# A causal convolution over matrices: the MID node's data sums on GpSimd, and x loaded into SBUF throughout

## Chip, cores and metric

The kernel runs on one core of one Trainium2 chip. The metric is the device time of one execution in microseconds, the median of its runs; lower is better. A core has TensorE (PE, matrix products), VectorE (DVE) and ScalarE (ACT) for elementwise work, GpSimd (POOL), SyncE (SP), and 16 DMA engines that all queues share. Each engine works through its own instructions in the order of the program, and waits on semaphores for the others.

## What is computed

```python
B, S, D, K = 8, 4096, 512, 8      # x: B,S,D   kernel: K,D,D   all float32
out = np.zeros_like(x)
for k in range(K):
    shifted = x moved down by k positions in S, zeros in front
    out += np.matmul(shifted, kernel[k])
```

Every output row is the sum of eight products of an input row with a 512x512 matrix.

## The kernel before

**Layout.** The 32768 rows are cut into 128 runs of 256 consecutive rows, one run per partition. A step takes K = 8 positions of every run, so there are 32 steps (i = 0 to 31). Products need the data transposed, with the 512 features on partitions: XT holds one step, positions 0 to 3 in its lower half and 4 to 7 in its upper half.

**Fewer products.** The convolution of eight taps is not done with 64 position-by-tap products per step. It is split three times into halves, and each split replaces four smaller products by three: one for the low part (LO), one for the high part (HI) and one for the sum of both (MID). A step so has three nodes, MID, LO and HI, and each node has nine products of 128x512 by 512x512 (four matmuls each). In return sums of data and of weights are needed. The weight sums are made once. The data sums are made in each step in bf16: D4, D41, D42, D421 for LO and HI, and D1, D2, D21 for the MID node. The last three are eleven blocks of 128x512: D1 two, D2 five, D21 four.

**Who makes the sums.** `tt` (L75) issues an add on VectorE. `prep_m` (L100) makes D1 and D2[1:5] from XT, `prep_d27` (L105) makes D2[0] = XT[5] + XT[7], and `prep_d21` (L108) makes D21 from D2. At the time of `prep_m` the upper half of XT still holds the step before and the lower half already holds the new one.

**How x arrives.** `load_x` (L86) loads one half step from DRAM, float32, cast to bf16, on GpSimd's DMA queue. In steps 0 to 2 it goes into SBUF tiles `xin` of a pool of two buffers. From step 3 on it goes into DRAM tiles `xd`. `transpose_x` (L91) is a DMA transpose on SP's queue from that tile into a half of XT.

**The order.** It is written out by hand (`manual_schedule`): the first six nodes, those of steps 0 and 1, line by line, and the rest (steps 2 to 31, 90 nodes) in the loop at the end. In the loop a node `cur` does its leaf products `node_l`, the earlier stages of the next node `nxt` (`node_a0`, `node_u`, `node_seed`, `node_dts`, `node_v`, `node_d`) are woven in, and `node_a1` of the node after that closes the pass. `node_l` of a MID node reads D21, `node_a1` and `node_a0` read D1, `node_u` reads XT[0] and `node_v` reads D2. `node_e` ends a node: for MID ScalarE copies the result into `ms`, for LO and HI VectorE adds or subtracts it into `y`, and SP stores `y`. The transposes of the next step stand at the start of MID (lower half) and at the end of LO (upper half), and the two loads for the step after that stand right behind the latter:

```python
        if a == LO and more:
            transpose_x(i + 1, 1)
            if i + 2 < NIT:
                load_x(i + 2, 0)
                load_x(i + 2, 1)
```

In XT, transposes wait for the readers of the half that they overwrite; the upper half is read by `prep_m`, `prep_d27` and `prep_d4`.

Of the kernel before, what the change touches and what calls it, by code (L numbers as in the profile page):

```python
# [22 lines left out]
def kernel(  # L23
# [6 lines left out]
    nc = tc.nc  # L30
    B, S, D = x.shape
    K = kernel.shape[0]
    P = 128
# [5 lines left out]
    bf = mybir.dt.bfloat16  # L39
# [12 lines left out]
    xpool = ctx.enter_context(tc.tile_pool(name="x", bufs=2))  # L52
# [22 lines left out]
    def tt(o, a, b, op):  # L75
        nc.vector.tensor_tensor(out=o, in0=a, in1=b, op=op)  # L76


    def load(out, src):
        nc.gpsimd.dma_start(out=out, in_=src)  # L80

    xin = {}

    dpool = ctx.enter_context(tc.tile_pool(name="xd", bufs=6, space=bass.MemoryType.DRAM))

    def load_x(i, h):  # L86
        pool = xpool if i < 3 else dpool
        xin[i, h] = pool.tile([P, 4, D], bf, name="xin" if i < 3 else "xd")
        load(xin[i, h], xr[:, K * i + 4 * h:K * i + 4 * h + 4, :])

    def transpose_x(i, h):  # L91
        nc.sync.dma_start_transpose(  # L92
            out=XT[:, 4 * h:4 * h + 4, :].rearrange("p j (c m) -> p (j c) m", m=P),
            in_=xin[i, h].rearrange("p j d -> p (j d)"))


    def pairs(z):
        return z.rearrange("p (a b) d -> p a (b d)", b=2)

    def prep_m():  # L100

        tt(D1[:, 0:2], XT[:, 7::-7], XT[:, 0:2], ADD)
        tt(pairs(D2[:, 1:5]), pairs(XT)[:, 3::-3], pairs(XT)[:, 0:2], ADD)

    def prep_d27():  # L105
        tt(D2[:, 0], XT[:, 5], XT[:, 7], ADD)

    def prep_d21():  # L108
        tt(D21[:, 0:4], D2[:, 0:4], D2[:, 1:5], ADD)

    def prep_d4(h):
        a, b = (XT[:, 4:8], XT[:, 0:4]) if h == LO else (XT[:, 0:4], XT[:, 4:8])
        tt(D4[:, 4 * h:4 * h + 4], a, b, ADD)

    def prep_d41(h):
        if h == LO:
            tt(D41[:, 0:2], D4[:, 7::-7], D4[:, 0:2], ADD)
        else:
            tt(D41[:, 2:4], D4[:, 3:5], D4[:, 4:6], ADD)

    def prep_d42(h):
        if h == LO:
            tt(pairs(D42)[:, 0:2], pairs(D4)[:, 3::-3], pairs(D4)[:, 0:2], ADD)
        else:
            tt(D42[:, 4:8], D4[:, 2:6], D4[:, 4:8], ADD)

    def prep_d421(h):
        if h == LO:
            tt(D421[:, 0:4:2], D42[:, 7:0:-6], D42[:, 0:4:2], ADD)
            tt(D421[:, 1:4:2], D42[:, 0:4:2], D42[:, 1:4:2], ADD)  # L130
        else:
            tt(D421[:, 4:8], D42[:, 3:7], D42[:, 4:8], ADD)
# [11 lines left out]
    H, HF = XT, D421.bitcast(f32).rearrange("p (t b) d -> p t (b d)", b=2)  # L144
    nc.sync.dma_start(out=HF, in_=xr[:, RUN - 4:RUN, :])
    load_x(0, 0)
    zero = spool.tile([P, D], bf, name="zero")
    nc.vector.memset(zero, 0.0)  # L148
# [90 lines left out]
    def node_a1(k):  # L239
        n = Node()  # L240
        nodes.append(n)
        n.k, (n.i, n.a) = k, order[k]
        a = n.a
        n.s = streams(n.i, a)
        n.q = pair(3)
        product(n.q[:, 1], n.s[1][1], W[a, MID, HI], True)
        nc.scalar.copy(out=n.q[:, 0], in_=n.q[:, 1])  # L247
        n.p = {}

    def node_a0(n):  # L250
        product(n.q[:, 0], n.s[1][0], W[n.a, MID, LO], False)

    def node_u(n):
        product(n.q[:, 1], n.s[0], W[n.a, MID, MID], False)

    def node_seed(n, b_):
        n.p[b_] = pair((2 * n.k + b_) % 3)
        if b_ == LO:
            nc.scalar.copy(out=n.p[b_][:, 1], in_=n.q[:, 1])  # L259
        else:  # L260
            nc.scalar.mul(out=n.p[b_][:, 1], in_=n.q[:, 1], mul=-1.0)  # L261

    def node_dts(n):
        n.dts = cpool.tile([P, D], f32, name="dts")
        nc.scalar.copy(out=n.dts, in_=n.q[:, 0])  # L265

    def node_v(n, b_):
        product(n.p[b_][:, 1], n.s[2][b_], W[n.a, b_, MID], False)

    def node_d(n, b_):  # L270
        p = n.p[b_]
        if b_ == LO:
            tt(p[:, 0], n.dts, p[:, 1], SUB)
        else:
            nc.vector.scalar_tensor_tensor(out=p[:, 0], in0=p[:, 1], scalar=-1.0,  # L275
                                           in1=n.dts, op0=MUL, op1=SUB)
# [3 lines left out]
    def node_l(n, b_, j):  # L280
        product(n.p[b_][:, j], n.s[3][2 * b_ + j], W[n.a, b_, j], False)
# [11 lines left out]
    def node_e(n, b_):  # L293
        p = n.p[b_]
        if n.k < 4:
            pool, name = ((mpool, "ms"), (ypool, "y"), (fpool, "f"), (ypool, "y"))[n.k]
            y = pool.tile([P, 2, D], f32, name=name)
            nc.scalar.copy(out=y, in_=p)
            first[n.i, n.a, b_] = y
        elif n.a == MID:  # L300
            ms[b_] = mpool.tile([P, 2, D], f32, name="ms")
            nc.scalar.copy(out=ms[b_], in_=p)  # L302
        else:
            y = ypool.tile([P, 2, D], f32, name="y")
            if b_ == HI and n.k == len(order) - 1:

                for j, eng in enumerate((nc.scalar, nc.sync)):
                    tt(y[:, j], p[:, j], ms[b_][:, j], ADD if n.a == LO else SUB)
                    eng.dma_start(out=orr[:, K * n.i + 4 * n.a + 2 * b_ + j, :], in_=y[:, j])
            else:  # L310
                tt(y, p, ms[b_], ADD if n.a == LO else SUB)
                store(n.i, n.a, b_, y)
# [54 lines left out]
    transpose_pe("he", 1, H, 1, 4)  # L367
    load_w(7)
    load_x(0, 1)
    nc.vector.tensor_copy(out=XF[:, 6:8], in_=bank["xb"])  # L370
    tt(D2, XF[:, 1:6], XF[:, 3:8], ADD)
    fill(pair(2))
    tt(D4[:, 2:4], XF[:, 2:4], XF[:, 6:8], ADD)
    load_x(1, 0)
    direct(0, 2)
    tt(to(E4[:, 1:4]), prev(bank["he"]), to(XF[:, 1:4]), ADD)
# [47 lines left out]
    node_u(nodes[1])  # L424
    node_e(nodes[0], 0)
    prep_d27()
    mid_dve(2, HI, LO)
    load_w(1)
# [88 lines left out]
    node_l(nodes[4], 0, LO)  # L517
    node_u(nodes[5])
    prep_m()
    node_d(nodes[4], 1)  # L520
    node_y(nodes[4], 0, LO)
# [8 lines left out]
    node_dts(nodes[5])  # L530
    node_v(nodes[5], 0)
    prep_d27()
    node_seed(nodes[5], 1)
    node_y(nodes[4], 1, LO)
# [42 lines left out]
    for k, (i, a) in enumerate(order):  # L577
        if k < 6:
            continue
        cur = nodes[k]  # L580
        more = i + 1 < NIT
        if a == MID and more:
            transpose_x(i + 1, 0)
        node_l(cur, 0, LO)
        node_l(cur, 0, HI)
        nxt = nodes[k + 1] if k + 1 < len(order) else None
        if nxt:
            node_a0(nxt)
            node_u(nxt)
        node_l(cur, 1, LO)  # L590
        node_e(cur, 0)
        if nxt:
            node_seed(nxt, 0)
            node_seed(nxt, 1)
            node_dts(nxt)
        if a == MID:
            prep_d421(LO)
            prep_d41(HI)
        elif a == LO:
            if more:  # L600
                prep_m()
            prep_d421(HI)
        elif more:
            prep_d41(LO)
            prep_d42(LO)
            prep_d21()
        if nxt:
            for b_ in range(2):
                node_v(nxt, b_)
                node_d(nxt, b_)  # L610
        if a == MID:
            prep_d42(HI)
            prep_d27()
        elif more:
            prep_d4(LO if a == LO else HI)
        node_l(cur, 1, HI)
        if k + 2 < len(order):
            node_a1(k + 2)
        node_e(cur, 1)
# [5 lines that stand above are left out]
# [30 lines left out]
```

## Time and profile before

| | before |
|---|---|
| median of 2 runs | 900.64 us (900.48 and 900.81) |
| the profiled execution | 900.81 us |
| its span | 898.7 us |
| mean granted clock of PE | 0.935 |
| PE busy | 771.2 us (86%) |
| VectorE busy | 658.0 us (73%) |
| ScalarE busy | 285.0 us (32%) |
| GpSimd busy | 41.4 us (5%) |
| DMA issues of xd | 58 of 512 KB |
| DMA transposes of XT | 3 from xin, 58 from xd |

The span runs from the first to the last instruction; the time includes what lies around it. Busy shares are means over the whole span, so they hide that stages differ; the row of 40 slices (each 22.5 us) and tables by stage show that. In a group's row the number behind the bar is the busy time in us and then the mean of one instruction in ns; behind the second bar stands the engine's idle time just before these instructions, with what ended it. A wait is written "who <- for whom: total us, times, longest us". "PEclk" is the clock that TensorE was granted, as a share of the full one.

### The profile page before, as it was taken

Reading aid. Unit: us, or ns where it says so; the run is one execution under the profiler, and the core shown is the slowest. Engines: PE = TensorE matmul, PEld = TensorE weight load, DVE = VectorE, ACT = ScalarE, POOL = GpSimd, SP = SyncE. Lnnn points to the kernel's source line nnn. Section 1 sums busy time; section 2 is a strip of 40 time slices with the busy share of each in tenths; the row PEclk is TensorE's granted clock in tenths of the full one; section 3 lists DMA queues with packets and bytes.
Section 4 is the critical chain, followed back from the end, with each engine's and each line's share of the span. In section 5 each row is a group of like instructions: output and inputs, shape, how many; then the busy total and the mean of one; then the engine's idle time right before and its main releaser. Section 6 shows DMA issues by size and latency. Waiting matters only on the chain.

```text
span 898.7 us, 9321 instructions
## 1 busy us (share of the span) xinstructions
PE 771.2 (86%) x3513; PEld 349.1 (39%) x3584; DVE 658.0 (73%) x766; ACT 285.0 (32%) x462; POOL 41.4 (5%) x80
## 2 busy tenths in 40 slices
PE   7980813106999999999999999999999999999997
PEld 3430301002444444444444444444444444444443
DVE  4970802006888888888888888888888888888886
ACT  3640200001333333333333333333333333333332
POOL 4032121110000000000000000000000000000000
PEclk9995865656999999999999999999999999999999
DMA  9999999999554444444455544454545444445553
GB/s 203 189 186 211 235 210 249 239 211 212 141 140 140 125 128 129 135 132 128 139 141 140 141 141 131 128 140 141 141 129 151 129 137 135 128 131 141 140 132 127
DMA packets 159374, 139.42 MB, mean 155 GB/s; under 512 B 130145, under 2 KB 134241, under 8 KB 159201
## 3 DMA queue, kind: packets, MB, share of 16 engines
q1 hardware_dynamic: 145456, 99.89, 40.1%
q0 software_dynamic: 13728, 38.67, 22.0%
q8 instruction: 28, 0.46, 0.2%
q10 hardware_dynamic: 144, 0.26, 0.1%
q14 instruction: 18, 0.14, 0.1%
HBM read 77.33 MB, written 97.52 MB: 195 GB/s over the span
## 4 chain that ended last, share of the span: by engine, by line
PE 75%; DMA 12%; another core or an unknown queue 5%; DVE 4%; SPq 2%; issue 1%; POOL 0%; ACT 0%; DVEq 0%; ACTq 0%; POOLq 0%
PE pp L200 74%; DMA XT<-xin 5%; DMA out_dram<-y 4%; DMA xin<-in_x_dram 2%; DVE D L76 2%; DMA XT<-xd 2%; DVE y L76 1%; SPq L92 1%; SPq L285 1%; DVE pp L76 0%; DVE pp L275 0%; POOL w L80 0%; ACT pp L259 0%; PE pp L189 0%
## 5 line engine op out<-in xcount | busy, mean ns | idle before, releaser
L200 PE MATMUL pp<-w,D 128*128 128x512 bf16 x3214 | 718.2, 381 | 88.8 <-DVE D L76 80.9
L200 PEld LDWEIGHTS <-D 128*128 128x128 bf16 x3280 | 321.7, 98 | 479.0 <-DVE D L76 84.0
L76 DVE TENSOR_TENSOR D<-XT 128x2048 bf16<-128x2048 bf16 (+2 forms) x153 | 142.4, 947 | 134.6 <-DMA XT<-xd 70.3
L76 DVE TENSOR_TENSOR D<-D 128x1024 bf16<-128x1024 bf16 (+1 forms) x252 | 228.4, 947 | 1.6 <-ACT D L356 1.6
L76 DVE TENSOR_TENSOR y<-pp,ms 128x1024 f32<-128x1024 f32 (+1 forms) x121 | 146.7, 1213 | 51.4 <-PE pp L200 44.0
L247 ACT COPY pp<-pp 128x512 f32<-128x512 f32 x95 | 54.1, 570 | 338.7 <-PE pp L200 335.9
L259 ACT COPY pp<-pp 128x512 f32<-128x512 f32 x95 | 54.1, 570 | 207.7 <-PE pp L200 196.1
L76 DVE TENSOR_TENSOR pp<-dts,pp 128x512 f32<-128x512 f32 x95 | 65.8, 692 | 34.8 <-ACT dts L265 33.1
L302 ACT COPY ms<-pp 128x1024 f32<-128x1024 f32 x60 | 61.0, 1016 | 33.1 <-PE pp L200 32.0
L275 DVE SCALAR_TENSOR_TENSOR pp<-pp,dts 128x512 f32<-128x512 f32 x95 | 66.1, 696 | 3.3
L265 ACT COPY dts<-pp 128x512 f32<-128x512 f32 x95 | 57.5, 605 | 2.0 <-PE pp L200 2.0
L261 ACT ACTIVATE pp<-pp 128x512 f32<-128x512 f32 x95 | 56.1, 590 | 2.7 <-DVE y L76 2.7
L80 POOL DMA_DIRECT2D xd<-in_x_dram x58 | 30.3, 552 | 122.5 <-DMA xd<-in_x_dram 117.5
L200 PE MATMUL pp<-w,F 128*128 128x512 bf16 x34 | 9.8, 413 | 28.5 <-DVE pp L275 28.4
L200 PE MATMUL pp<-w,XT 128*128 128x512 bf16 x118 | 30.6, 380 | 0.3 <-issue 0.2
L76 DVE TENSOR_TENSOR w<-w,w 128x2048 bf16<-128x2048 bf16 x18 | 21.7, 1222 | 0.3 <-DMA w<-in_kernel_dram 0.3
L200 PEld LDWEIGHTS <-XT 128*128 128x128 bf16 x120 | 11.8, 99 | 14.5 <-issue 0.7
L200 PEld LDWEIGHTS <-F 128*128 128x128 bf16 x36 | 3.8, 104 | 33.5 <-issue 30.0
L200 PE MATMUL pp<-w,w 128*128 128x512 bf16 x36 | 9.0, 378 | 1.3 <-ACT pp L247 0.7
L183 PE MATMUL pp<-zero 128*128 128x512 bf16 x23 | 8.0, 479 | 2.4 <-DVE zero L148 1.2
L341 DVE MEMSET D<- 128x64 bf16 x2 | 0.2, 112 | 8.1 <-ACT D L354 7.6
L80 POOL DMA_DIRECT2D w<-in_kernel_dram x8 | 6.1, 770 | 0.6 <-DMA w<-in_kernel_dram 0.6
(56 smaller groups left out, 75.2 us busy)
## 6 DMA issues: line engine op xcount, KB each, us to landing
out_dram<-y SPq DMA_DIRECT2D x123, 512.0 KB, 3.3
xd<-in_x_dram POOLq DMA_DIRECT2D x58, 512.0 KB, 21.2
w<-in_kernel_dram POOLq DMA_DIRECT2D x8, 512.0 KB, 15.9
xin<-in_x_dram POOLq DMA_DIRECT2D x6, 512.0 KB, 13.6
D<-in_x_dram SPq DMA_DIRECT2D x1, 1024.0 KB, 4.8
out_dram<-ms SPq DMA_DIRECT2D x2, 512.0 KB, 18.4
out_dram<-f SPq DMA_DIRECT2D x2, 512.0 KB, 20.7
XT<-xd SPq DMA_TRANSPOSE x58, 5.4
```

Of the source, the lines that this page charges most:

```text
L76: nc.vector.tensor_tensor(out=o, in0=a, in1=b, op=op)
L80: nc.gpsimd.dma_start(out=out, in_=src)
L92: nc.sync.dma_start_transpose(out=XT[:, 4 * h:4 * h + 4, :].rearrange("p j (c m) -> p (j c) m", m=P), in_=xin[i, h].rearrange("p j d -> p ...
L183: nc.tensor.matmul(pw[:, h], lhsT=zero[:, 0:P], rhs=zero, start=True, stop=True)
L200: nc.tensor.matmul(bank, lhsT=comp[:, c * P:(c + 1) * P], rhs=w[:, c, :], start=start and c == 0, stop=c == DC - 1, skip_group_check=True)
L247: nc.scalar.copy(out=n.q[:, 0], in_=n.q[:, 1])
L259: nc.scalar.copy(out=n.p[b_][:, 1], in_=n.q[:, 1])
L261: nc.scalar.mul(out=n.p[b_][:, 1], in_=n.q[:, 1], mul=-1.0)
L265: nc.scalar.copy(out=n.dts, in_=n.q[:, 0])
L275: nc.vector.scalar_tensor_tensor(out=p[:, 0], in0=p[:, 1], scalar=-1.0, in1=n.dts, op0=MUL, op1=SUB)
L285: nc.sync.dma_start(out=orr[:, t0:t0 + 2, :], in_=y)
L302: nc.scalar.copy(out=ms[b_], in_=p)
```

## The change

Two edits. First, the DRAM pool is gone and all loads of x go to the SBUF tiles `xin` (two buffers). Second, in the loop `prep_m`, `prep_d21` and `prep_d27` are called with `tg`, which issues the same add on GpSimd; in the first six nodes they stay on VectorE. The place of each call in the order is kept.

```diff
-    dpool = ctx.enter_context(tc.tile_pool(name="xd", bufs=6, space=bass.MemoryType.DRAM))
-
     def load_x(i, h):
-        pool = xpool if i < 3 else dpool
-        xin[i, h] = pool.tile([P, 4, D], bf, name="xin" if i < 3 else "xd")
+        xin[i, h] = xpool.tile([P, 4, D], bf, name="xin")
         load(xin[i, h], xr[:, K * i + 4 * h:K * i + 4 * h + 4, :])
...
-    def prep_m():
-
+    def tg(o, a, b, op):
+        nc.gpsimd.tensor_tensor(out=o, in0=a, in1=b, op=op)
+
+    def prep_m(tt=tt):
         tt(D1[:, 0:2], XT[:, 7::-7], XT[:, 0:2], ADD)
...
-    def prep_d27():
+    def prep_d27(tt=tt):
...
-    def prep_d21():
+    def prep_d21(tt=tt):
...
             if more:
-                prep_m()
+                prep_m(tg)
             prep_d421(HI)
         elif more:
             prep_d41(LO)
             prep_d42(LO)
-            prep_d21()
+            prep_d21(tg)
...
         if a == MID:
             prep_d42(HI)
-            prep_d27()
+            prep_d27(tg)
```

## Prediction

> **What bounds the kernel now.** I read the page's 40 slices first. One slice is 22.5 us.
>
> ```profile
> PE   7980813106999999999999999999999999999997
> ...
> DVE  4970802006888888888888888888888888888886
> ...
> POOL 4032121110000000000000000000000000000000
> PEclk9995865656999999999999999999999999999999
> DMA  9999999999554444444455544454545444445553
> ```
>
> There are two kernels in this row. From slice 11 (225 us) to the end PE is full at the full clock, VectorE is at 80 to 89%, GpSimd is empty and the DMA engines are half used: that part is bound by PE. Before it, in slices 4 to 10, PE is mostly idle while the DMA engines are saturated. The waits of the first 240 us (who <- whom: total, times, longest) say for whom PE idled:
>
> ```profile
> PE pp L200 <- DVE D L76: 80.9, 2, 46.9
> DVE D L76 <- DMA XT<-xin: 64.2, 2, 34.8
> ...
> DVE D L76 <- DMA XT<-xd: 50.5, 2, 48.7
> ...
> PE pp L200 <- DVE pp L275: 28.4, 1, 28.4
> ```
>
> PE waits for VectorE's sums, and these wait for the DMA transposes that fill XT. Together with two small waits of PE (1.3 us for ACT L261, 1.2 us for DVE L76) that is 111.8 us. Why the transposes are late stands in the timeline of that stretch (start, duration, engine):
>
> ```profile
> 39.37 27.97 SPq L92 DMA_TRANSPOSE XT<-xin  x2
> ...
> 44.09 1.23 DVE L76 TENSOR_TENSOR D<-XT 128x2048 bf16<-128x2048 bf16 x1
> ...
> 45.62 3.47 POOL L80 DMA_DIRECT2D xd<-in_x_dram  x6
> ...
> 197.91 0.52 POOL L80 DMA_DIRECT2D xd<-in_x_dram  x1 [2.15 <-DMA xd<-in_x_dram]
> ```
>
> From 45.62 to 197.91 us GpSimd issues all 58 loads into xd, one each 2.67 us, as fast as they land: nothing makes a load wait for the step that uses it. The transpose issued at 39.37, before this flood, has landed when VectorE reads XT at 44.09: 4.7 us. Those issued in the flood took up to 60 us.
>
> Next, one steady step. Time zero of a step is the copy L247 at 502.20, at which PE turns from HI to MID:
>
> ```profile
> 502.20 0.57 ACT L247 COPY pp<-pp 128x512 f32<-128x512 f32 x1 [2.80 <-PE pp L200]
> ...
> 505.75 2.46 SPq L92 DMA_TRANSPOSE XT<-xd  x1
> ...
> 517.99 1.22 DVE L76 TENSOR_TENSOR y<-pp,ms 128x1024 f32<-128x1024 f32 x1
> ...
> 519.67 3.21 SPq L92 DMA_TRANSPOSE XT<-xd  x1
> ```
>
> The lower half's transpose leaves 3.5 us into the step; the upper half's leaves 17.5 us into it, behind the store of y (517.99) on SP's queue. Where VectorE waited for it, it landed 5.6 us (566.93 to 572.51), 5.7 us and once 7.4 us after its issue. The step lasts 23.37 us (SP's y stores from 512.90 to 863.51: 15 steps), each of its three nodes 7.8 us.
>
> **The change, part by part.**
>
> *No xd buffers.* All loads go back to the two SBUF buffers xin, one for each half. A load must now wait until the transpose of the step before has read its buffer, so the flood can't form, and the first six steps' transposes should land as the one at 39.37 did. That returns the 111.8 us of PE's idling, and the slow clock after each idle stretch: PE restarts at a granted clock of 0.5, for 4.2 us (93.5 to 97.7), 5.9 us (149.4 to 155.3) and some 7 busy us (208.5 to 217), of which half is lost, 8.5 us. 898.7 - 111.8 - 8.5 = 778 us would be the span with a steady loop as now. VectorE stood idle in all of these waits, so I expect little to appear behind them; if the three early transposes showed 5 us each, it would be 793.
>
> *VectorE loses four instructions a step*: D2[0] (0.42 us), D1 (0.68), D2 (1.22) and D21 (1.22), 3.5 us of some 20. In the steady loop PE sets the pace, so this is worth nothing.
>
> *GpSimd gets them, in the order of the program.* Its queue per step becomes D2[0], D1, D2, load of the lower half, load of the upper half, D21. The price is not in the trace. Its nearest rows:
>
> ```profile
> L76 DVE TENSOR_TENSOR D<-D 128x2048 bf16<-128x2048 bf16 x123 | 147.4, 1218 | 0.0
> ...
> masks.py:199 POOL TENSOR_SCALAR_AFFINE_SELECT ident<-ident 128x128 bf16<-128x128 bf16 x1 | 0.3, 287 | 0.1
> ```
>
> Floor: VectorE's 1.22 us for the same shape. From GpSimd's own row: 16 x 287 ns = 4.6 us if all of it scales, 3.1 us if the 98 ns of a one-element memset there are fixed (98 + 16 x 189). That select reads one operand and the sum reads two, so I take the upper end, 4.6 us; D1 then costs 2.3, D2[0] 1.15, in all 12.65 us a step.
>
> The Trainium skill (GPSIMD Engine Reference, Performance versus the Vector engine) gives 4497 ns for a two-input add of 2048 float32 elements per partition, about twice VectorE; with that in place of 4.6 us, the sum below would be 3 us lower. No run here has shown it yet.
>
> *D2[0], D1 and D2 are covered.* With the lower half's transpose as now (landed 9 us into the step) D1 ends at 11.3 and D2 at 15.9. D1 is first used by PE at 14.7, D2 in the HI node (20), and the upper half's transpose, which may not overwrite XT[7] before D2 has read it, leaves at 17.5. If that cover of 1.6 us is gone, each us more is a us per step.
>
> *D21 is not covered: this is the new wait.* The load of the upper half, for two steps ahead, waits on GpSimd for the upper half's transpose to land. Behind it in the queue stands D21, and PE's first product of the next MID node reads D21. Before, VectorE made D21 early in the HI node, waiting for nothing of this. The new chain from one MID start to the next: 17.5 (transpose issued) + 5.6 (landed) + 0.55 (load issued; xin row 0.57, median 0.54) + 4.6 (D21) = 28.25 us against 23.37. PE idles 4.9 us in each step, and as the chain starts at PE's MID node again, it repeats; nothing catches up. The last loads are issued in step 29, so MID nodes 3 to 30 wait: 28 times.
>
> *The clock.* What an idle PE costs after the wait, the trace shows in rows of 1 us (length, PE, PEld, DVE, ACT, POOL, granted clock):
>
> ```profile
> 65.00:66.00 1.00, 0.17 (x1) 0.00 (x0) 0.00 (x0) 0.00 (x0) 0.52 (x1) 1.00 1.07 211
> ...
> 69.00:70.00 1.00, 0.00 (x0) 0.00 (x0) 0.00 (x0) 0.00 (x0) 0.00 (x0) 0.98 1.06 209
> 70.00:71.00 1.00, 0.00 (x0) 0.00 (x0) 0.00 (x0) 0.00 (x0) 0.16 (x1) 0.50 1.08 214
> ```
>
> PE stops at 65.2 and the clock halves at 70.0: 4.8 us. At the two other stalls it took 2.5 us (115.4 to 117.9) and 3.8 us (161.7 to 165.5). A gap of 4.9 us is just over all three. A halved clock costs 2.1 us (4.2 at half) to 2.9 us (5.9 at half); I take 2.5 us in three gaps of four, 1.9 us a step; bounds 0 and 2.9.
>
> *Sum.* 28 x (4.9 + 1.9) = 190 us; 778 + 190 = 968 us of span. The profiled execution took 900.81 us for a span of 898.7, so 2 us lie around it, and it is 0.2 us over the median of the runs: 970 us.
>
> A rule that speaks against the change beyond this: the Trainium skill (SBUF — State Buffer, Who interferes with whom) says that a VectorE instruction with two SBUF inputs and a GpSimd instruction that reads SBUF exclude each other, the later one waiting for the whole of the earlier. VectorE's D4 sum of the upper half is released by the same transpose as GpSimd's load, so D21 would start after its 1.22 us instead of 0.55 us; by that rule the time would be 28 x 0.67 = 19 us more, 989. No row of before has both engines reading, so the trace can't say.
>
> **The rivals.**
>
> *GpSimd's sum is cheap (faster).* All hangs on D21's price. At VectorE's 1.22 us the chain is 24.9 us, 1.5 us over the step, too short to halve the clock: 778 + 28 x 1.5 + 2 = 822 us. At 3.1 us PE idles 3.4 us, which one of the three stalls would have punished: 28 x (3.4 + 0.8) gives 898. Break-even is (900.6 - 780) / 28 = 4.3 us per step, clock included. For it: 287 ns is one short instruction with its start in it. Against it: two operands. Faster by over 2% needs a price below about 2.6 us, or a transpose from SBUF that lands at 4.6 us together with a price below 3.6.
>
> *GpSimd and VectorE hold each other up (slower still).* VectorE reads two SBUF operands for over 8 us of each step and GpSimd would for 12.65. If they don't overlap, D21 starts at least 0.7 us later, every gap halves the clock, and D2's cover is eaten: 28 x (4.9 + 0.7 + 2.5) gives 1007 us. Against: the sum of some 21 us still fits into a step of 30.
>
> *PE keeps its clock (about the same to slower).* If 4.9 us are not enough, as the 4.8 us at 65 us nearly were, 28 x 4.9 gives 917 us.
>
> *The loop stays bound by PE (faster).* If the load didn't hold GpSimd's queue, D21 would be early and the time 780 us. In the program built from the changed kernel the load stands ahead of D21 with a wait for that transpose, so I give this little.
>
> **How the numbers follow.** My forecast (930 to 990) 0.46; both engines hold each other up 0.23; clock kept 0.13; GpSimd cheap 0.14; loop bound by PE 0.04. A change of 2% is about what a measurement of this kernel can tell from none; it is 883 to 919 us here. Faster by over 2%: 0.15 (most of the cheap case, and the last). Within 2%: 0.11 (half of the clock's case, the rest of the cheap one). Slower by over 2%: 0.74. The range for eight in ten, 890 to 1020, reaches from a price near 3 us to both engines in each other's way.
>
> **What would show it.** Right: GpSimd busy near half of the loop; the xin loads spread over the whole span; slices 4 to 10 full for PE; then one gap of some 5 us per step, "PE waits for POOL D21", in front of each MID node; a period near 30 us; PEclk below 9 all along. D21's row near 4600 ns decides the price. Wrong: PE at 99% in the loop with no wait for GpSimd, or a time below 883 us; also a loop that waits for D1 or for the transpose of the lower half, or PE idle before 225 us as now.

## The result

The changed kernel takes 989.46 us (median of 2 runs, 988.8 and 990.13) against 900.64 us before: a ratio of 1.0986, 95% interval 1.0939 to 1.1033, so 10% slower. Its span is 987.0 us. The start and the loop changed in opposite directions, as the prediction said. The slices of the changed kernel, now 24.7 us each:

```profile
PE   7999688988879888899788898888888889888898
...
DVE  5999679667676766866677766776777776677766
...
POOL 3103534345433454234542345523455233552450
PEclk9999789988899888998888988889888898888989
DMA  9966676456565565645657446574565655557533
```

PE and its clock are full in slices 2 to 4 (to 99 us); the old kernel began to idle at 65 us. From slice 5 on PE is below 90% in 29 of 36 slices, its granted clock falls with it, and GpSimd works throughout. The waits from 90 us to the end say what PE waits for:

```profile
PE pp L199 <- POOL D L98: 129.3, 28, 8.8
PEld L199 <- issue: 99.8, 365, 0.3
```

PE waited 28 times for a GpSimd sum, 4.6 us each on average. The second row is the slow clock: weight loads that follow each other too late, at the half clock's pace, 13 in each step. One step in the timeline of the changed kernel (selected rows):

```profile
498.01 3.20 SPq L89 DMA_TRANSPOSE XT<-xin  x1
...
503.06 1.23 DVE L76 TENSOR_TENSOR D<-XT 128x2048 bf16<-128x2048 bf16 x1
503.50 0.53 POOL L80 DMA_DIRECT2D xin<-in_x_dram  x1 [14.73 <-PE pp L199]
504.05 4.15 POOL L98 TENSOR_TENSOR D<-D 128x2048 bf16<-128x2048 bf16 x1
...
504.20 1.22 DVE L76 TENSOR_TENSOR y<-pp,ms 128x1024 f32<-128x1024 f32 x1
505.33 5.57 DVE L76 TENSOR_TENSOR D<-D 128x1024 bf16<-128x1024 bf16 x3
...
508.25 21.05 PE L199 MATMUL pp<-w,D 128*128 128x512 bf16 x82 [4.26 <-POOL D L98]
...
528.50 3.24 SPq L89 DMA_TRANSPOSE XT<-xin  x1
...
534.01 0.53 POOL L80 DMA_DIRECT2D xin<-in_x_dram  x1 [15.01 <-PE pp L199]
```

This is the chain of the prediction, row by row: the upper half's transpose (498.01), the load that had to wait for it (503.50), D21 behind the load (504.05 to 508.20), PE's first MID product (508.25), and 20.25 us later the next transpose. The profile names PE as the load's releaser here, but the transpose is the better reading: the load starts 0.44 us after VectorE's D4 sum, which reads what the transpose wrote, and in the first gap, where the profile names the transpose for both, the distance is the same (D4 at 105.73, the load at 106.18). From the transpose at 130.17 to the one at 958.40, 27 steps, a step lasts 30.68 us.

The granted clock of the same gap, in rows of 1 us (the clock is the third number from the end):

```profile
506.00:507.00 1.00, 0.00 (x0) 0.00 (x0) 1.00 (x1) 0.00 (x0) 1.00 (x1) 0.99 1.11 205
507.00:508.00 1.00, 0.00 (x0) 0.00 (x0) 1.00 (x1) 0.00 (x0) 1.00 (x1) 0.50 0.99 193
...
513.00:514.00 1.00, 1.00 (x4) 0.35 (x3) 0.00 (x0) 0.00 (x0) 1.00 (x1) 0.59 0.00 0
```

PE stopped at 503.99. The clock fell 3.0 us later and came back at 513.8, so PE worked 5.6 us at half speed.

VectorE's three sums at 505.33 take 5.57 us here and 1.89 us in the old kernel. The groups say the same in the mean (ns of one behind the busy time); first the old kernel's row, then the changed kernel's:

```profile
L76 DVE TENSOR_TENSOR D<-D 128x1024 bf16<-128x1024 bf16 x127 | 81.8, 684 | 1.6 <-ACT D L356 1.6
```

```profile
L76 DVE TENSOR_TENSOR D<-D 128x1024 bf16<-128x1024 bf16 x127 | 184.9, 1493 | 1.6 <-ACT D L355 1.6
...
L98 POOL TENSOR_TENSOR D<-D 128x2048 bf16<-128x2048 bf16 x29 | 121.0, 4174 | 0.5
L98 POOL TENSOR_TENSOR D<-XT 128x2048 bf16<-128x2048 bf16 x29 | 118.8, 4096 | 0.0
...
L98 POOL TENSOR_TENSOR D<-XT 128x1024 bf16<-128x1024 bf16 x29 | 61.5, 2120 | 96.4 <-DMA XT<-xin 86.0 <-PE pp L199 10.4
```

GpSimd's price for 2048 elements is 4.1 to 4.2 us. VectorE's 1024-element sum, 684 ns before, is 1493 ns in the mean without any change to it. The y at 504.20 lies inside the same GpSimd sum and takes its usual 1.22 us. It reads one operand from PSUM (`pp`), the stretched sums read both from SBUF.

### The profile page after: what moved, and what is told of

Its sections match the earlier page's. It is cut to its first block, busy times and chain, and to the rows that moved or that the text cites. A ratio compares the mean times of both kernels' runs of the same rounds, so it can differ in the third digit from the quotient of the medians.

```text
span 987.0 us, 9440 instructions
## 1 busy us (share of the span) xinstructions
PE 841.2 (85%) x3513; PEld 363.9 (37%) x3584; DVE 710.1 (72%) x649; ACT 285.6 (29%) x462; POOL 386.6 (39%) x197
## 4 chain that ended last, share of the span: by engine, by line
PE 61%; DMA 17%; POOL 14%; DVE 4%; issue 3%; SPq 1%; ACT 0%; POOLq 0%; DVEq 0%
PE pp L199 61%; DMA XT<-xin 15%; POOL D L98 12%; DVE y L76 4%; DMA xin<-in_x_dram 2%; POOL xin L80 2%; SPq L284 1%; POOL w L80 0%; PE pp L188 0%; DVE D L76 0%; SPq L89 0%; ACT y L297 0%; DVE pp L76 0%; DVEq L649 0%; ACT pp L258 0%
## 5 line engine op out<-in xcount | busy, mean ns | idle before, releaser
L199 PE MATMUL pp<-w,D 128*128 128x512 bf16 x3214 | 790.2, 407 | 135.3 <-POOL D L98 129.3
L199 PEld LDWEIGHTS <-D 128*128 128x128 bf16 x3280 | 337.0, 104 | 582.5 <-POOL D L98 142.8
L76 DVE TENSOR_TENSOR D<-D 128x1024 bf16<-128x1024 bf16 (+1 forms) x223 | 329.4, 1510 | 1.6 <-ACT D L355 1.6
L98 POOL TENSOR_TENSOR D<-XT 128x512 bf16<-128x512 bf16 (+2 forms) x88 | 223.8, 2557 | 111.6 <-DMA XT<-xin 96.4
L80 POOL DMA_DIRECT2D xin<-in_x_dram x64 | 35.4, 553 | 465.8 <-PE pp L199 346.5
L98 POOL TENSOR_TENSOR D<-D 128x2048 bf16<-128x2048 bf16 x29 | 121.0, 4174 | 0.5
L76 DVE TENSOR_TENSOR D<-XT 128x2048 bf16<-128x2048 bf16 (+2 forms) x65 | 79.2, 1221 | 10.9 <-DMA XT<-xin 9.0
```

Source lines behind the costliest of these rows:

```text
L98: nc.gpsimd.tensor_tensor(out=o, in0=a, in1=b, op=op)
L199: nc.tensor.matmul(bank, lhsT=comp[:, c * P:(c + 1) * P], rhs=w[:, c, :], start=start and c == 0, stop=c == DC - 1, skip_group_check=True)
```

## The experiments

Two questions: is the loss really D21's place behind the load, and what do the stretched VectorE sums mean?

### All sums back on VectorE

```diff
-                prep_m(tg)
+                prep_m()
...
-            prep_d21(tg)
+            prep_d21()
...
-            prep_d27(tg)
+            prep_d27()
```

> The changed kernel with all MID sums back on VectorE; x still goes through the two SBUF buffers. Theory (the flood of early loads was what cost the old kernel its first 225 us, and the SBUF buffers end it): 787 us minus little, that is 778 us of span worked out from the old profile, 780 us of time, PE at 99% from about 45 us on, step 23.4 us. Rival (the two SBUF buffers themselves delay the loop, by a later load or a slower transpose): the step stays above 24 us and the time above 800.

Measured: 779.77 us, ratio to before 0.8656 (0.8636 to 0.8676), span 778.1 us.

```profile
PE   7999999999999999999999999999999999999997
...
PEclk9999999999999999999999999999999999999999
```

The step is 23.33 us. So the SBUF buffers alone gain 120 us, and the sums on GpSimd lose 210 on top of them (beside the DRAM buffers they lose some 14, as the last experiment shows). This kernel also beats both of the pair.

### D21 alone back on VectorE

```diff
-            prep_d21(tg)
+            prep_d21()
```

> The changed kernel with D21 alone back on VectorE; D1, D2 stay on GpSimd. Theory (D21 behind the load of the upper half is the whole stall): nothing waits behind that load any more that PE needs at once, step back to 23.4 to 24 us, 780 to 800 us. Rival (GpSimd's and VectorE's sums exclude each other, and this is what costs): seven of the eleven blocks are still on GpSimd, so some 7/11 of the 7.3 us per step stay, 28 x 4.7 = 130 us, time near 910.

Measured: 859.07 us (0.9543; 0.9513 to 0.9572), step 26.07 us, between the two expectations: 130 us of the loss are gone and 79 us stay. PE no longer waits for GpSimd. The LO node of a step shows what stays:

```profile
507.70 6.14 POOL L98 TENSOR_TENSOR D<-XT 128x1024 bf16<-128x1024 bf16 x2 [8.54 <-DMA XT<-xin]
...
510.30 4.63 DVE L76 TENSOR_TENSOR D<-XT 128x2048 bf16<-128x2048 bf16 x1
...
514.85 2.34 DVE L76 TENSOR_TENSOR y<-pp,ms 128x1024 f32<-128x1024 f32 x2
516.14 0.57 ACT L258 COPY pp<-pp 128x512 f32<-128x512 f32 x1 [4.11 <-DVE y L76]
```

VectorE's D4 sum is ready at 510.30 while GpSimd adds D1 and D2 (to 513.84). It takes 4.63 us instead of 1.22 and ends 1.1 us after GpSimd does, about its own length: I read this as standing still until GpSimd was done. Both y behind it are late, ScalarE's seed waits for y, and PE for the seed.

### The load moved behind D21

```diff
                 load_x(i + 2, 0)
-                load_x(i + 2, 1)
...
             prep_d21(tg)
+            if i + 2 < NIT:
+                load_x(i + 2, 1)
```

> The changed kernel with one line moved: the load of the upper half stands behind D21 in GpSimd's queue instead of ahead of it. All eleven sums stay on GpSimd at the same price. Theory (place in the queue): D21 then starts when D2 and the lower load are done, some 16 us into the step, is ready at 20, before PE needs it at 23.4; step 23.4 to 24.5 us, 780 to 815 us. Rival (the price of GpSimd's sums, 12 us a step, or the exclusion of the two engines): the step stays above 28 us, time above 915.

Measured: 860.19 us (0.955; 0.9526 to 0.9575), step 26.08 us. One line moved, with every sum still on GpSimd, gives back 129 us, so place in the queue was most of the loss. The theory's full recovery did not come. Waits between 300 and 800 us:

```profile
ACT pp L258 <- DVE y L76: 90.6, 35, 4.3
...
PE pp L199 <- ACT pp L258: 24.5, 31, 2.3
```

It is the late y again. With D21 on VectorE or on GpSimd the time is the same (859 and 860 us) once D21 does not stand behind the load, though the load's place differs too.

### GpSimd busy, but reading next to nothing

The kernel with D21 on VectorE, with fills in place of GpSimd's D1 and D2, so that it leaves out those two sums and its output is not the convolution:

```diff
-                prep_m(tg)
+                tg(D1[:, 0, 0:64], XT[:, 7, 0:64], XT[:, 0, 0:64], ADD)
+                nc.gpsimd.memset(D1[:, 1], 0.0)
+                for _ in range(2):
+                    nc.gpsimd.memset(D2[:, 1:5], 0.0)
```

> The kernel with D21 alone on VectorE (859 us), but on GpSimd the sums D1 and D2[1:5] are replaced by one 64-element add (so that it still waits for the transpose of the lower half) and by fills with zeros, D2 twice, about as long as the sums or a little shorter: D1 and D2 are then not the reference's. GpSimd is busy in the same place and writes the same tiles but reads next to nothing. Theory (a VectorE sum of two SBUF operands stands still while a GpSimd sum reads SBUF): the D4 sum of the LO node falls from 4.6 to 1.2 us, step 23.4 to 23.8 us, 780 to 793 us. Rival (D2 is late for PE, or GpSimd's place in the queue delays a load): the step stays near 26 us, 850 to 860 us.

Measured: 803.77 us (0.8917; 0.888 to 0.8954), above the 780 to 793 expected. GpSimd is occupied for some 5 us here, against 6.1, in the same place, and VectorE's sums no longer stretch. A D4 sum that lies wholly within the fills, and the groups:

```profile
524.82 3.66 POOL L603 MEMSET D<- 128x2048 bf16 x2
...
526.83 1.22 DVE L76 TENSOR_TENSOR D<-XT 128x2048 bf16<-128x2048 bf16 x1
```

```profile
L76 DVE TENSOR_TENSOR D<-D 128x2048 bf16<-128x2048 bf16 x123 | 147.3, 1217 | 0.0
...
L603 POOL MEMSET D<- 128x2048 bf16 x58 | 104.7, 1804 | 1.7
...
L76 DVE TENSOR_TENSOR D<-XT 128x2048 bf16<-128x2048 bf16 x62 | 76.6, 1235 | 60.9 <-DMA XT<-xin 60.9
```

The D<-XT sums were 2570 ns in the kernel with D21 on VectorE. But 24 us over the kernel with all sums on VectorE remain, and the last row gives a reason to test: VectorE waits 60.9 us for transposes.

### The same, with the lower load ahead of the fills

```diff
             if more:
+                if i + 2 < NIT:
+                    load_x(i + 2, 0)
                 tg(D1[:, 0, 0:64], XT[:, 7, 0:64], XT[:, 0, 0:64], ADD)
...
-                load_x(i + 2, 0)
                 load_x(i + 2, 1)
```

> The kernel whose GpSimd only fills D1 and D2 with zeros (804 us; D1 and D2 not the reference's), with the load of the lower half moved ahead of the fills, to the point at which the transpose of the lower half has landed. Theory (a load that runs shortly before or beside the upper half's transpose delays it, and that is the 20 us which this kernel had over the one with all sums on VectorE): VectorE's wait for the transposes falls from 39 us in 500 to below 15, step 23.4, 780 to 788 us. Rival (the fills themselves, or their writes, cost it): 798 to 808 us.

Measured: 779.08 us (0.8654; 0.864 to 0.8669), and of VectorE's wait for the transposes between 300 and 800 us this is left:

```profile
DVE D L76 <- DMA XT<-xin: 2.0, 2, 1.5
```

These 25 us came from where the load stood. The upper half's transpose now lands after 5.0 us in the median, against 6.5 us before the load was moved (issues between 250 and 720 us). So the way from 859 to 779 us has two parts: 55 us go when GpSimd no longer reads (and is a little sooner done), 25 us when the load stands elsewhere; then nothing is lost against the kernel with all sums on VectorE. Moving the load was not tried beside real sums with D21 on VectorE.

### PE kept busy in the gap

```diff
-        product(n.q[:, 1], n.s[1][1], W[a, MID, HI], True)
+        for _ in range(6 if a == LO and n.i > 2 else 1):
+            product(n.q[:, 1], n.s[1][1], W[a, MID, HI], True)
```

> The changed kernel, but the product a1 of each LO node from step 3 on is made six times instead of once (the repeats write the same result), so that PE works 4.3 us where it would wait for D21. Theory on the clock (the wait halves TensorE's clock for some 5 us of each step, worth 2.5 to 2.7 us): granted clock back to 1.0 in the loop, step 30.7 - 2.6 = 28.1 us, time 989 - 28 x 2.6 = 916 us, although PE does 5 x 4 x 29 = 580 matmuls more. Rival (the halved clock lies beside the chain and costs nothing): time stays at 985 to 995.

Measured: 970.65 us (1.0775; 1.0734 to 1.0816), mean granted clock 0.994. One step:

```profile
501.17 18.42 PE L199 MATMUL pp<-w,D 128*128 128x512 bf16 x83 [1.78 <-POOL D L98]
...
518.83 3.20 SPq L89 DMA_TRANSPOSE XT<-xin  x1
...
526.07 0.53 POOL L80 DMA_DIRECT2D xin<-in_x_dram  x1 [14.18 <-DMA XT<-xin]
```

The clock's part is as expected: from PE's start to the transpose it is 17.66 us instead of 20.25, 2.6 us less, with 580 more matmuls run. In 26 of its 28 gaps, now 1.6 to 2.0 us long, the clock stayed full. But of those 2.6 us a step, 1.75 were lost again: the load starts 7.24 us after the transpose's issue instead of 5.5. The DMA issues of the changed kernel and of this one, at that place, with the time to landing at the end:

```profile
XT<-xin SPq DMA_TRANSPOSE x1, 5.0
```

```profile
XT<-xin SPq DMA_TRANSPOSE x1, 6.7
```

### The same, with the lower load earlier

```diff
             if more:
+                if i + 2 < NIT:
+                    load_x(i + 2, 0)
                 prep_m(tg)
...
-                load_x(i + 2, 0)
                 load_x(i + 2, 1)
```

> The changed kernel with a1 made six times (971 us), with the load of the lower half moved ahead of D1 in GpSimd's queue. Theory (the same: the load of the lower half, which ended 1 to 2 us before the upper half's transpose was issued, is why it landed after 6.7 us instead of 5.0): it lands after 5.0 us again, 28 x 1.7 = 48 us less, 920 to 930 us. Rival (the transposes are late for another reason): 965 to 975 us.

Measured: 999.11 us (1.1095; 1.1079 to 1.1112): worse, and my theory on the load falls for this kernel. The transpose still lands after 6.7 us. Instead D1 and D2 now start 5.8 us after PE's MID start, not 4.1, and hold up VectorE's D42 sum for longer (4.42 us before):

```profile
518.77 6.14 POOL L98 TENSOR_TENSOR D<-XT 128x1024 bf16<-128x1024 bf16 x2
...
519.87 6.13 DVE L76 TENSOR_TENSOR D<-D 128x2048 bf16<-128x2048 bf16 x1
```

The D42 sum stood still for 5 us behind them, and y, the seed and PE with it. Why transposes land after 5.0 us in some kernels and 6.7 in others stays open.

### Half of D21 on GpSimd

```diff
-            prep_d21(tg)
+            tg(D21[:, 0:2], D2[:, 0:2], D2[:, 1:3], ADD)
+            tt(D21[:, 2:4], D2[:, 2:4], D2[:, 3:5], ADD)
```

> The changed kernel with D21 made half on GpSimd (blocks 0 and 1) and half on VectorE (blocks 2 and 3). Theory (the chain through D21 sets the step and the clock halves only after 2.5 to 4.8 us without work): 2.1 us less on GpSimd leaves a gap of 2.2 us, in which the clock is kept in most steps: step 30.7 - 2.1 - 2.6 = 26.0 us, 781 + 28 x 2.6 + 2 = 856 us, granted clock above 0.97. Rival (the clock does not depend on the length of the gap): only the 2.1 us are saved, 28 x 5.2 more than 783 us, 929 us, clock near 0.9.

Measured: 914.98 us (1.0133; 1.0087 to 1.018), step 28.10 us, granted clock 0.944. Neither number holds. Between 300 and 800 us, in 18 steps:

```profile
PE pp L199 <- POOL D L98: 53.0, 18, 5.3
PEld L199 <- issue: 34.8, 122, 0.9
```

The gap is 2.9 us in the mean, not 2.2, and reaches 5.3 in one step. Late weight loads are 7 a step against 13 in the changed kernel (211 in 16 steps of the same stretch), so the price of the slow clock does depend on the gap. The granted clock of the whole run, gap by gap, shows what my theory had wrong. It fell in all 10 gaps of 3 us or more and in 12 of the 18 shorter ones (2.3 to 3.0 us); in 8 of these it fell only after PE had started again. So the clock can fall after a gap that is already over. What the length changes is how long the clock stays at half: 6.83 us or more for the seven gaps of 4 us and over, 3.41 us for the other 15.

### The old DRAM buffers, with the sums on GpSimd

```diff
-                prep_m()
+                prep_m(tg)
...
-            prep_d21()
+            prep_d21(tg)
...
-            prep_d27()
+            prep_d27(tg)
```

(in the old kernel)

> The old kernel with only the second half of the change: the eleven sums on GpSimd, x still through DRAM buffers from step 3 on. No load waits for a transpose there, but GpSimd's sums stand between the loads in its queue. Theory: the flood is gone because the sums hold the loads back (PE idle before 225 us falls from 112 us to under 30), D21 waits for no transpose, and what is left is the two engines keeping each other from reading: a step near 26 us, 850 to 880 us. Rival (the flood comes from the DRAM buffers themselves): PE again idles some 110 us at the start, and the time is above 960 us.

Measured: 915.4 us (1.0159; 1.013 to 1.0188), step 28.25 us. The slices show the flood gone:

```profile
PE   7999899888897987998988898988979898888988
```

In slices 2 to 10 PE is at 80% and more. So the flood took both: DRAM buffers that no load has to wait for, and a GpSimd queue with nothing else in it. Either half of the change alone ends it. The step is 2 us longer than I expected. GpSimd holds up two sums of the LO node here (D421 of 3.11 us at 513.95, and D4):

```profile
516.98 4.07 POOL L101 TENSOR_TENSOR D<-D 128x2048 bf16<-128x2048 bf16 x1
...
518.18 3.97 DVE L76 TENSOR_TENSOR D<-XT 128x2048 bf16<-128x2048 bf16 x1
```

and half of the upper transposes land only after some 9 us or more. The two were not told apart.

## Why the prediction was right, point by point

**The base.** 778 us of span without the flood was worked out from the old profile; the kernel with all sums on VectorE has 778.1. No transpose showed behind the waits, so the 793 us were not needed. One reading behind it was off: the first restart ran at half clock until 97.3 us (the row from 97 to 98 us has 0.87), 3.7 us and not 4.2, which moves the base by 0.2 us.

**The new wait.** Place, cause and count were right: 28 waits for D21, and moving one load gives 129 us back. Two of the signs were put too simply: slices 4 to 10 could not all be full, as the loop with its gaps begins in slice 5, and the clock's slices alternate between 8 and 9.

**The chain's terms.** Load issued after the transpose's issue: predicted 5.6 us, measured 5.5. Load: 0.55 and 0.53. D21: predicted 4.6, measured 4.17; scaling a one-operand row to a two-operand sum overshot by 0.4. The gap of 4.9 us was 4.6, in all 7 us less.

**The clock** is the mis-sized term. I charged 2.5 us in three gaps of four, 1.9 us a step, because 4.9 us lay just over the three delays that I had read between PE's stop and the slow clock. In the changed kernel the clock fell in all 28 gaps, 2.1 to 3.5 us after PE's stop, and stayed at half for 6.83 us (10.24 in the first), so that PE worked 3.5 to 6.0 us of it at half speed. PE is busy for 841.2 us here and for 762.4 us with all sums on VectorE: 78.8 us more, or 2.8 us a step. With that the sum closes: 778.1 + 129.3 (the waits for D21) + 78.8 = 986.2 of the 987.0 us.

**How near it came.** The two errors, 7 us too much for the gap and 26 us too little for the clock, partly cancelled, and 989.5 us lies at the very top of the forecast's 930 to 990. The rival of two engines in each other's way had the clock right (2.5 us in every gap) and its 0.7 us at D21 wrong.

**The rule on reading.** The Trainium skill (SBUF — State Buffer, Who interferes with whom) says that a VectorE sum of two SBUF operands and a GpSimd instruction that reads SBUF exclude each other, and that one that only writes does not disturb. The runs agree with both parts: 4.63 instead of 1.22 us beside GpSimd's sums, 1.22 us beside its fills. In this kernel the rule hardly reached the chain, where I had priced it at 0.67 us: VectorE's D4 sum starts 0.44 us ahead of the load, so D21 behind the load finds it nearly done, and D21 takes 4.17 us in the mean against 4.10 for D2 of the same size. That the prediction's sum with the rule came to 989 is therefore chance. The long stops of VectorE fall into PE's wait. But it is the larger part of what is left once that wait is gone: up to 55 of the 79 us, as the fills also ended about 1 us sooner than the sums.

**VectorE's relief** was worth nothing, as said: 779.8 us without it, bound by PE.

## What to carry to other kernels

A load that waits for a buffer, issued from the queue of a computing engine, is a wait for everything behind it: put work that another engine needs soon ahead of it. Sums given to a second engine can stop the first one's: look at the mean duration of the *unchanged* instructions, which tells it at once. And a recurring gap of some microseconds on TensorE can cost more than its own length: here 4.6 us of waiting drew 2.8 us of slow clock behind it, and gaps of 2.3 us sometimes drew it too.

## What the hardware showed that I had not expected

- VectorE's lost time is not shown as waiting but as longer instructions: 128x1024 sums of 684 ns are 1493 ns in the mean, and a pair or triple that is merged in the timeline shows one long span.
- GpSimd adds bf16 at about 2 ns an element per partition (2120 ns for 1024, 4.07 to 4.17 us for 2048), and fills 2048 bf16 in 1.80 us.
- The upper half's transpose of 512 KB lands after 5.0 us in the median in some kernels (the changed one, all sums on VectorE, half of D21) and after 6.4 to 6.7 us in others (D21 on VectorE, the load behind D21, PE kept busy). One cause was found (a load shortly before it, worth 24.7 us in the kernel with fills), and one case where moving that load changed nothing.
- Every half-speed stretch of the clock, in all runs, lasted a whole multiple of 3.41 us (3.41, 6.83 and 10.24 in the loops; 27.3, 37.5 and 51.2 in the old kernel's three stalls), but for the last one of each run, which the run's end cuts off. So a gap's price does not grow evenly with its length.
